# Turning 32 images by 90 degrees: the first group loaded in longer rows and turned like the others

## The chip, the core and the metric

The kernel runs on one core of a Trainium2 chip. The metric is the device time of one execution in microseconds. Three runs of the kernel before took 122.88 to 123.08 us, with a median of 122.94.

## What is computed

```python
def setup_inputs():
    batch, c, h, w = 32, 3, 256, 256
    return {"x": np.random.randn(batch, c, h, w).astype(np.float32)}

def reference(x):
    return np.rot90(x, k=-1, axes=(-2, -1)).astype(np.float32)
```

There are 96 images (32 x 3) of 256 x 256 float32, each turned by a quarter: row i of the result is column i of the image, read from the last row to the first. 25.17 MB come in and 25.17 MB go out, and nothing is calculated.

## The kernel before

**Tiling.** All images together are 24,576 rows of 256 numbers. They are cut into twelve units of 2 MB (128 partitions x 16 rows) and these into five groups, `sizes = (2, 2, 2, 4, 2)` (L38): groups 0, 1, 2 and 4 hold 4 MB each, group 3 holds 8 MB. Each group has a tile `u` of its own in the on-chip memory (L40), which is filled once, turned in place and stored. Nothing is used twice except three small holding areas of 1 MB: `spare[0]` and `spare[1]` in PSUM (L45) and `extra` (L46).

**Loads** are issued on SP's queue, 14 in all. Groups 1 to 4 (L57 to L66) are loaded so that a partition gets whole runs of 16 image rows (32 for group 3), 16 KB (32 KB) in one piece, from each of two halves `a`. A load covers every I-th partition (`to[i::I]`), where I is the group's size: 64 partitions of 128 for I = 2. The last load of the last group is issued as two of 1 MB (L63, L64), and `mark` is the first of them. Group 0 is different (L52 to L56): it is two slabs of 2 MB, in which each partition gets 8 rows, 8 KB, of each of two image sets. Slab 0 comes first, as two loads of 1 MB over all 128 partitions (L55), then slab 1 in one load of 2 MB (L56).

**The turn.** VectorE's transpose swaps blocks of 32 partitions x 32 elements. The loads put an image's rows so that with these blocks and a suitable access pattern the whole quarter turn is done in one pass. Each instruction handles 128 x 2048 elements, and there are 24. In `turn_group` (L80) the tile is split in four quarters (low and high halves of column and row): the first quarter is transposed into a holding area (L88), three more are transposed within the tile, each into the place that the one before it has left (L93), and at the end ScalarE copies the held quarter back (L98). All of them read and write all 128 partitions and both halves `a`. The holding areas are `extra` for group 1, `spare[1]` for group 2, both `spare` for group 3 and `extra` for group 4 (L100). In group 0, `turn_slab` (L68) turns a slab with two transposes: slab 0 into `spare[0]` and `spare[1]` (L75), then slab 1 into the place of slab 0 (L76), and ScalarE copies the two spares into the place of slab 1 (L78).

**Stores** are issued on SP's queue too, two for each group, over the even and the odd partitions (L106 for group 0, L113 for the others): rows of 16 KB, 2 MB each, 4 MB each for group 3.

**The order of the work** is the program's order on each engine; the framework adds the waits that the data need. SP issues all loads and then all stores, in the order of the groups. One dependency is added by hand (L108): the first store waits until the load `mark` has landed, so that stores don't run beside loads, except for the last 1 MB. VectorE takes the groups in order, as do ScalarE's copies.

Of the kernel before, what the change touches and what calls it, by code (L numbers as in the profile page):

```python
# [1 line left out]

# [4 lines left out]


@with_exitstack  # L10
def kernel(
    ctx: ExitStack,
    tc: tile.TileContext,
    x: bass.AP,
    out: bass.AP,
):

    nc = tc.nc
    fp32 = mybir.dt.float32

    B, C, H, W = x.shape
    P = nc.NUM_PARTITIONS
    R = 16  # L30
    E = R * W
    hw = R // 2
    low, high = slice(0, hw), slice(hw, R)

    rows_in = x.rearrange("b c h w -> (b c h) w")
    rows_out = out.rearrange("b c h w -> (b c h) w")

    sizes = (2, 2, 2, 4, 2)  # L38
    first = [sum(sizes[:n]) for n in range(len(sizes))]
    groups = [  # L40
        ctx.enter_context(tc.tile_pool(name=f"group{n}", bufs=1)).tile([P, s, E], fp32, name=f"u{n}")
        for n, s in enumerate(sizes)
    ]
    psum = ctx.enter_context(tc.tile_pool(name="psum", bufs=1, space=bass.MemoryType.PSUM))
    spare = [psum.tile([P, E // 2], fp32, name=f"spare{h}") for h in range(2)]  # L45
    extra = ctx.enter_context(tc.tile_pool(name="extra", bufs=1)).tile([P, E // 2], fp32, name="extra")  # L46

    def rows_of(rows, n):
        return rows[first[n] * P * R : (first[n] + sizes[n]) * P * R]


    ld = rows_of(rows_in, 0).rearrange("(s i p r) w -> s i p (r w)", s=2, i=2, p=P)  # L52
    home = [groups[0][:, s].rearrange("p (i f) -> p i f", i=2) for s in range(2)]
    for i in range(2):
        nc.sync.dma_start(out=home[0][:, i], in_=ld[1, i])  # L55
    nc.sync.dma_start(out=home[1], in_=ld[0].transpose([1, 0, 2]))  # L56
    for n in range(1, len(sizes)):  # L57
        I = sizes[n]
        ld = rows_of(rows_in, n).rearrange("(a i m r) w -> i m a (r w)", a=2, i=I, m=P // I)
        to = groups[n].rearrange("p s f -> p (s f)").rearrange("p (a f) -> p a f", a=2)  # L60
        for i in range(I):
            if (n, i) == (len(sizes) - 1, I - 1):
                mark = nc.sync.dma_start(out=to[i::I, 0], in_=ld[i][:, 0])  # L63
                nc.sync.dma_start(out=to[i::I, 1], in_=ld[i][:, 1])  # L64
            else:
                nc.sync.dma_start(out=to[i::I], in_=ld[i])  # L66

    def turn_slab(src, dsts):  # L68
        s = src.rearrange("p (i r g c) -> p c r g i", i=2, r=R // 2, c=R)
        for h, d in enumerate(dsts):  # L70
            d = d.rearrange("p (c k r) -> p c r k", c=hw, r=R // 2)[:, :, ::-1, ::-1]
            nc.vector.transpose(out=d, in_=s[:, h * hw : (h + 1) * hw])  # L72

    u = groups[0]
    turn_slab(u[:, 0], spare)  # L75
    turn_slab(u[:, 1], [u[:, 0, : E // 2], u[:, 0, E // 2 :]])  # L76
    for h in range(2):
        nc.scalar.copy(out=u[:, 1, h * E // 2 : (h + 1) * E // 2], in_=spare[h])  # L78

    def turn_group(n, held):  # L80
        I = sizes[n]
        T = I // 2
        K = W // (R * T)
        u = groups[n].rearrange("p s f -> p (s f)")
        src = u.rearrange("p (a t r g c) -> p t c r g a", a=2, t=T, r=R, c=R)
        dst = u.rearrange("p (i c k t r) -> p t c r k i", i=I, c=R, k=K, t=T)[:, ::-1, :, ::-1, ::-1, :]
        for t in range(T):
            nc.vector.transpose(  # L88
                out=held[t].rearrange("p (i c k r) -> p c r k i", i=I, c=hw, k=K)[:, :, ::-1, ::-1, :],
                in_=src[:, t, low, low])  # L90
        for c, r in ((low, high), (high, high), (high, low)):
            for t in range(T):
                nc.vector.transpose(out=dst[:, t, c, r], in_=src[:, t, c, r])  # L93
        back = u.rearrange("p (i c k t r) -> p t i c k r", i=I, c=R, k=K, t=T)[:, ::-1]
        for t in range(T):
            kept = held[t].rearrange("p (i c k r) -> p i c k r", i=I, c=hw, k=K)
            for i in range(I):
                nc.scalar.copy(out=back[:, t, i, low, :, high], in_=kept[:, i])  # L98

    for n, held in enumerate(([extra], [spare[1]], spare, [extra]), 1):  # L100
        turn_group(n, held)


    st = rows_of(rows_out, 0).rearrange("(s i m r) w -> i m s (r w)", s=2, i=2, m=P // 2)
    for a in range(2):
        put = nc.sync.dma_start(out=st[a], in_=groups[0][a::2])  # L106
        if a == 0:
            tc.add_manual_dep(put.ins, mark.ins.name, mybir.DependencyInfo(  # L108
                mybir.DependencyClass.Sync, mybir.DependencyReason.SCHED_ONLY), reason="stores after loads")
    for n in range(1, len(sizes)):  # L110
        st = rows_of(rows_out, n).rearrange("(a i m r) w -> a m i (r w)", a=2, i=sizes[n], m=P // 2)
        for a in range(2):
            nc.sync.dma_start(out=st[a], in_=groups[n][a::2])  # L113


# [1 line left out]
_INS = ['x']  # L117
_OUTS = [((32, 3, 256, 256), 'float32')]


# [23 lines left out]
```

## Time and profile before

| | us |
|---|---|
| median of three runs | 122.94 |
| profiled execution, its own time | 122.88 |
| its span, first to last instruction | 121.1 |
| VectorE busy, 24 transposes | 87.4 |
| ScalarE busy, copies and a table load | 14.9 |
| GpSimd busy | 0.2 |
| group 0: two transposes to `spare` (L72) | 7.1 |
| group 0: two transposes within `u` (L72) | 7.8 |
| group 0: two copies from `spare` (L78) | 3.6 |
| issue of one load of 1 MB, 128 rows of 8 KB (L55) | 0.38 to 0.42 |
| issue of one load of 1 MB, 64 rows of 16 KB (L63, L64) | 0.51, 0.50 |
| SP waits for `mark` ahead of the first store (L106) | 31.2 |

TensorE does nothing, and the clock granted is 1.0. The profile's page gives busy time by engine, the span in 40 slices, the DMA queues, the chain that ended last and the costliest groups of instructions. In a line of a group, "L93 DVE ... x15 | 54.4, 3649 | 0.4" means: line 93, VectorE, 15 instructions, 54.4 us in all, 3649 ns for one, 0.4 us of idle time ahead of them. DVE is VectorE, ACT ScalarE, SP the engine whose queue (SPq) issues all transfers here. "mean busy share" of the DMA line is that of 16 DMA engines. An issue on the queue is only the handing over of a transfer; its packets move later, and the trace has a record of each packet (start, duration, size).

### The profile page before, as it was taken

The page shows a single profiled execution, that of the slowest core. Times are in us where ns is not written, and L with a number is a line of the kernel's source. Part 1 is how long each engine was busy: PE and PEld are TensorE (multiplying, and loading weights), DVE is VectorE, ACT ScalarE, POOL GpSimd, SP SyncE. Part 2 cuts the span into 40 slices and gives each one's busy share as a digit, 9 for nine tenths or more (in the row PEclk, how much of TensorE's full clock was granted, in tenths as well). Part 3 has the DMA queues.
Part 4 walks back from the last instruction along what each step waited for, and adds up shares of the span by engine and source line. Part 5 has one row for each costly group of instructions (what it writes and reads, how often), then busy time and mean ns, then how long its engine had stood idle before and what let it go on. Part 6 is the DMA issues. An engine that isn't in the chain of part 4 may idle for free.

```text
span 121.1 us, 131 instructions
## 1 busy us (share of the span) xinstructions
DVE 87.4 (72%) x24; ACT 14.9 (12%) x17; POOL 0.2 (0%) x4
## 2 busy tenths in 40 slices
DVE  0039999999999999999999999999999600000000
ACT  0000400380005100060000000318000330000000
POOL 0000000000000000000000000000000000000000
DMA  2999999999989898999999999999999999999994
GB/s 89 428 428 422 452 433 433 433 433 433 520 346 520 346 520 346 428 422 411 433 433 428 433 433 428 417 417 433 428 433 433 433 433 433 433 433 433 433 422 184
DMA packets 3456, 50.33 MB, mean 416 GB/s; under 512 B 384, under 2 KB 384, under 8 KB 384
## 3 DMA queue, kind: packets, MB, share of 16 engines
q1 hardware_dynamic: 3456, 50.33, 97.6%
HBM read 25.17 MB, written 25.17 MB: 416 GB/s over the span
## 4 chain that ended last, share of the span: by engine, by line
DVE 66%; issue 6%; DMA 6%; ACT 1%; ACTq 1%; SPq 0%; DVEq 0%
DVE u L93 39%; DVE spare L88 9%; DVE extra L88 6%; DVE u L72 6%; DVE spare L72 6%; DMA u<-in_x_dram 6%; ACT u L98 1%; ACTq L139 1%; SPq L55 0%; DVEq L88 0%; DVEq L72 0%
## 5 line engine op out<-in xcount | busy, mean ns | idle before, releaser
L93 DVE STREAM_TRANSPOSE u<-u 128x2048 f32<-128x2048 f32 x15 | 54.4, 3649 | 0.4
L72 DVE STREAM_TRANSPOSE spare<-u 128x2048 f32<-128x2048 f32 x2 | 7.1, 3586 | 8.1 <-DMA u<-in_x_dram 8.1
L98 ACT COPY u<-spare 128x512 f32<-128x512 f32 (+1 forms) x10 | 6.0, 687 | 38.5 <-DVE u L93 38.5
L88 DVE STREAM_TRANSPOSE spare<-u 128x2048 f32<-128x2048 f32 x3 | 10.7, 3588 | 0.0
L72 DVE STREAM_TRANSPOSE u<-u 128x2048 f32<-128x2048 f32 x2 | 7.8, 3988 | 0.0
L88 DVE STREAM_TRANSPOSE extra<-u 128x2048 f32<-128x2048 f32 x2 | 7.8, 3896 | 0.0
L98 ACT COPY u<-extra 128x1024 f32<-128x1024 f32 x4 | 4.0, 1043 | 22.8 <-DVE u L93 22.8
L78 ACT COPY u<-spare 128x2048 f32<-128x2048 f32 x2 | 3.6, 1870 | 8.7 <-DVE u L72 8.7
L78 ACT ACT_TABLE_LOAD x1 | 1.3, 1283 | 13.0 <-DMA u<-in_x_dram 13.0
L128 POOL MEMSET const-uint8-127<- 128x1 uint8 x1 | 0.1, 103 | 0.0
L128 POOL MEMSET const-bfloat16-1.0<- 128x1 bf16 x1 | 0.1, 102 | 0.0
L128 POOL MEMSET const-float32-0.0<- 128x1 f32 x1 | 0.1, 99 | 0.2 <-issue 0.2
L128 POOL MEMSET const-float32-1.0<- 128x1 f32 x1 | 0.1, 99 | 0.0
## 6 DMA issues: line engine op xcount, KB each, us to landing
u<-in_x_dram SPq DMA_DIRECT2D x10, 2048.0 KB, 30.4
out_dram<-u SPq DMA_DIRECT2D x8, 2048.0 KB, 18.2
out_dram<-u SPq DMA_DIRECT2D x2, 4096.0 KB, 21.1
u<-in_x_dram SPq DMA_DIRECT2D x4, 1024.0 KB, 20.5
```

Source lines behind the costliest of these rows:

```text
L72: nc.vector.transpose(out=d, in_=s[:, h * hw : (h + 1) * hw])
L78: nc.scalar.copy(out=u[:, 1, h * E // 2 : (h + 1) * E // 2], in_=spare[h])
L88: nc.vector.transpose(out=held[t].rearrange("p (i c k r) -> p c r k i", i=I, c=hw, k=K)[:, :, ::-1, ::-1, :], in_=src[:, t, low, low])
L93: nc.vector.transpose(out=dst[:, t, c, r], in_=src[:, t, c, r])
L98: nc.scalar.copy(out=back[:, t, i, low, :, high], in_=kept[:, i])
L128: nc = _bacc.Bacc("TRN2", target_bir_lowering=False, num_devices=1)
L139: with _tile.TileContext(nc) as tc:
```

## The change

Group 0 loses its own layout, its own turn and its own stores, and goes through the code of the other groups. Its loads are rows of 16 KB on every second partition: the first half `a` of the even partitions (1 MB, 64 partitions), the second half of them (1 MB), and the odd partitions (2 MB). It is turned by `turn_group` with `spare[0]` as the holding area: one transpose to `spare[0]`, three within the tile, two copies of 128 x 1024 by ScalarE. The dependency on `mark` moves into the common loop of stores.

```diff
-    ld = rows_of(rows_in, 0).rearrange("(s i p r) w -> s i p (r w)", s=2, i=2, p=P)
-    home = [groups[0][:, s].rearrange("p (i f) -> p i f", i=2) for s in range(2)]
-    for i in range(2):
-        nc.sync.dma_start(out=home[0][:, i], in_=ld[1, i])
-    nc.sync.dma_start(out=home[1], in_=ld[0].transpose([1, 0, 2]))
-    for n in range(1, len(sizes)):
+    for n in range(len(sizes)):
         I = sizes[n]
         ld = rows_of(rows_in, n).rearrange("(a i m r) w -> i m a (r w)", a=2, i=I, m=P // I)
         to = groups[n].rearrange("p s f -> p (s f)").rearrange("p (a f) -> p a f", a=2)
         for i in range(I):
-            if (n, i) == (len(sizes) - 1, I - 1):
+            if (n, i) in ((0, 0), (len(sizes) - 1, I - 1)):
                 mark = nc.sync.dma_start(out=to[i::I, 0], in_=ld[i][:, 0])
                 nc.sync.dma_start(out=to[i::I, 1], in_=ld[i][:, 1])
             else:
                 nc.sync.dma_start(out=to[i::I], in_=ld[i])
-
-    def turn_slab(src, dsts):
-        s = src.rearrange("p (i r g c) -> p c r g i", i=2, r=R // 2, c=R)
-        for h, d in enumerate(dsts):
-            d = d.rearrange("p (c k r) -> p c r k", c=hw, r=R // 2)[:, :, ::-1, ::-1]
-            nc.vector.transpose(out=d, in_=s[:, h * hw : (h + 1) * hw])
-
-    u = groups[0]
-    turn_slab(u[:, 0], spare)
-    turn_slab(u[:, 1], [u[:, 0, : E // 2], u[:, 0, E // 2 :]])
-    for h in range(2):
-        nc.scalar.copy(out=u[:, 1, h * E // 2 : (h + 1) * E // 2], in_=spare[h])
...
-    for n, held in enumerate(([extra], [spare[1]], spare, [extra]), 1):
+    for n, held in enumerate(([spare[0]], [extra], [spare[1]], spare, [extra])):
         turn_group(n, held)
...
-    st = rows_of(rows_out, 0).rearrange("(s i m r) w -> i m s (r w)", s=2, i=2, m=P // 2)
-    for a in range(2):
-        put = nc.sync.dma_start(out=st[a], in_=groups[0][a::2])
-        if a == 0:
-            tc.add_manual_dep(put.ins, mark.ins.name, ...)
-    for n in range(1, len(sizes)):
+    for n in range(len(sizes)):
         st = rows_of(rows_out, n).rearrange("(a i m r) w -> a m i (r w)", a=2, i=sizes[n], m=P // 2)
         for a in range(2):
-            nc.sync.dma_start(out=st[a], in_=groups[n][a::2])
+            put = nc.sync.dma_start(out=st[a], in_=groups[n][a::2])
+            if (n, a) == (0, 0):
+                tc.add_manual_dep(put.ins, mark.ins.name, ...)
```

## The prediction

> **What bounds the kernel now.** I read the page first: busy time, the line of the DMA engines in 40 slices, the queue, and the groups of instructions.
>
> ```profile
> span 121.1 us, 131 instructions
> ## 1 busy us (share of the span) xinstructions
> DVE 87.4 (72%) x24; ACT 14.9 (12%) x17; POOL 0.2 (0%) x4
> ...
> DMA  2999999999989898999999999999999999999994
> ...
> q1 hardware_dynamic: 3456, 50.33, 97.6%
> ...
> L93 DVE STREAM_TRANSPOSE u<-u 128x2048 f32<-128x2048 f32 x15 | 54.4, 3649 | 0.4
> ```
>
> The DMA engines are full from the second slice to the last: 97.6% of 121.1 us is 118.2 us of packets. VectorE has 87 us of work, starts late and is done 25 us before the end. So the time is start-up, plus 118 us of transfer, plus an end, plus any moment in which the queue runs dry. There is none now. The chain that ended last gives VectorE 66%; that is how stores are linked back to transposes and not what sets the end, since after the last copy at 97.9 us the DMA engines still move for 22 us.
>
> The windows view (length, then busy time of VectorE, ScalarE and GpSimd, clock, DMA share, GB/s) shows start and steady state:
>
> ```profile
> 0.73:1.73 1.00, 0.00 (x0) 0.00 (x0) 0.00 (x0) 1.00 0.00 0
> 1.73:2.38 0.65, 0.00 (x0) 0.00 (x0) 0.00 (x0) 1.00 0.37 50
> 2.38:2.90 0.52, 0.00 (x0) 0.00 (x0) 0.00 (x0) 1.00 0.88 347
> 2.90:12.20 9.30, 4.13 (x2) 0.00 (x0) 0.00 (x0) 1.00 1.01 428
> 14.00:31.00 17.00, 16.90 (x6) 3.92 (x3) 0.00 (x0) 1.00 1.01 432
> ```
>
> The first issue is at 0.73 us, the first packets at 1.73, all sixteen engines run from about 2.8. The 8 KB rows (2.9 to 12.2 us) go at 428 GB/s, the 16 KB rows after them at 432 (431 in the same view from 62 to 90 us, for stores). Last come the timelines of VectorE and of the queue on SP (start, length), which show how early each step is done:
>
> ```profile
> 8.06 7.08 DVE L72 STREAM_TRANSPOSE spare<-u 128x2048 f32<-128x2048 f32 x2 [8.06 <-DMA u<-in_x_dram]
> 15.18 7.82 DVE L72 STREAM_TRANSPOSE u<-u 128x2048 f32<-128x2048 f32 x2
> 22.84 3.91 DVE L88 STREAM_TRANSPOSE extra<-u 128x2048 f32<-128x2048 f32 x1
> 26.78 10.93 DVE L93 STREAM_TRANSPOSE u<-u 128x2048 f32<-128x2048 f32 x3
> 37.60 3.59 DVE L88 STREAM_TRANSPOSE spare<-u 128x2048 f32<-128x2048 f32 x1
> 41.23 10.93 DVE L93 STREAM_TRANSPOSE u<-u 128x2048 f32<-128x2048 f32 x3
> 52.12 7.08 DVE L88 STREAM_TRANSPOSE spare<-u 128x2048 f32<-128x2048 f32 x2
> ```
>
> ```profile
> 59.43 1.37 SPq L106 DMA_DIRECT2D out_dram<-u  x2
> ...
> 84.25 2.06 SPq L113 DMA_DIRECT2D out_dram<-u  x2
> ```
>
> VectorE never rests from 8.06 to 95.9 us (its transposes sat idle 0.4 us in all ahead of L93, the last column above), so whatever delays its start delays every later group. The 8 MB of group 3 are ready at 84.2 us, and its store is issued at 84.25.
>
> **The change, part by part.**
>
> *Bytes and rows.* The loads of group 0 stay three, of 1, 1 and 2 MB, so the queue, its 14 loads, its 10 stores and the order of their waits stay. Only the packets differ: 512 of 8 KB become 256 of 16 KB. The trace's packet records have 309 ns for the one and 613 for the other; 512 x 309 / 16 = 9.89 us against 256 x 613 / 16 = 9.81. That is on the path: **-0.08 us**.
>
> *Start-up.* SP issues the first load in 377 ns (L55, 128 rows of 8 KB); the same form as the new one, 64 rows of 16 KB on every second partition, is L63 and L64, with 505 and 495. If the first packet waits for the issue to end, everything is 0.12 us later. On the other side, the sixteen engines get their first packets from 1.73 to 2.80 us, four at once and twelve from 2.39; if that spread is the time in which 128 rows are described, 64 rows would need half of it, and the last engine would start 0.5 us earlier. The bounds are -0.5 and +0.2 us (two such issues). I take **+0.12**, since it is a duration of the very form, and what the spread is made of isn't shown.
>
> The Trainium skill speaks against the shape: "DMA: Bandwidth & Descriptors", Rules for kernel authors, wants 128 partitions for full bandwidth and says that transfers to disjoint halves of the partitions aren't worth splitting. Here the loads after 14 us are all of 64 or 32 partitions and move 432 GB/s, more than the 428 of the 128-partition loads; by the rule the first 4 MB would be slower, by these rows they aren't, and the rows decide.
>
> *ScalarE.* Two copies of 128x2048 out of PSUM (1.87 us each) go, two of 128x1024 (1.01 us on the same kind of tile) come. ScalarE is 12% busy and group 0's stores wait until 59.4 us for the loads in any case: nothing. Without that cover a copy would count a microsecond.
>
> *VectorE: the start.* Now the first transpose needs slab 0 alone, the first two loads; it starts at 8.06 us, 0.1 after they have landed. The in-place turn reads all 128 partitions and both halves of the row in its first transpose, so it needs all three loads, which have landed at 12.94 (ScalarE's first wait and SP's next issue end there). VectorE starts at 13.04. Behind that wait stand all 24 transposes. Their number stays. Group 0 then has the form of group 2 (one transpose into PSUM, three in place), which takes 52.12 - 37.60 = 14.52 us, so group 1 begins at 27.56 instead of 22.84: **4.7 us later**, with data there since 22.5. Nothing later makes it up, as VectorE has no idle time. The buffers don't add a wait: spare[0] is free again by 31 us and next wanted at 57, spare[1] keeps its two users and their distance.
>
> *Who waits for that.* Groups 0, 1 and 2 are ready at about 30, 45 and 59 us; their stores go out from 59.43, held by the loads. Group 2 is fourth to sixth in line (63.8 and later): covered. Group 4 is ready at 102.6 instead of 97.9 and its packets begin at 109.9: covered by 7 us. **Group 3** is the one to look at. Its store is issued at 84.25 + 4.71 = 88.96 us. The packets before it end at 90.33 on the first engine and 90.49 on the last (loads end at 61.1 to 61.3; 12.58 MB of stores at 431 GB/s are 29.2 us). Now the store is there 6.1 us ahead; after the change 1.37 to 1.53 us. (What shifts all transfers alike shifts landing and need alike, and drops out.)
>
> Is that enough to feed sixteen engines? No store in this trace meets an idle queue, so the price is bounded. From below: zero, if issue to packet is like the first packet of the whole kernel, 1.73 - 0.73 = 1.0 us. From above: the last engine at the start got its packet 2.80 - 0.73 = 2.07 us after the issue, which would leave 2.07 - 1.37 = 0.7 us dry; with an issue of 0.64 us rather than 0.38, about 0.95. A closer row is the turn from loads to stores: the first store was issued at 59.43, and every engine went from its last load straight on to it at 61.0 to 61.3, with 10 ns between. So a store reaches each engine within 1.57 to 1.83 us, and the most that can be missing by that row is 1.83 - 1.37 = 0.46. I take the late side of this row, as twelve of sixteen engines took 1.66 us and more at the start: 1.66 to 1.83 against 1.37 to 1.53, **+0.3 us**. It is not caught up, since each engine is full from there to the end.
>
> The Trainium skill gives some 0.6 us to the first byte for a transfer issued by SP ("DMA: Bandwidth & Descriptors", Latency and other measured facts). Added to an issue of 0.64 us that would be an estimate of 1.24 us, so no gap at all and about 122.9; this trace's 1.0 us for the first four engines agrees with it, and its 1.66 to 2.07 for the others doesn't.
>
> *Sum.* -0.08 + 0.12 + 0.3 = +0.34 on the profiled execution's 122.88 us (span 121.1 and 1.8 around it) gives 123.2; the median of the runs shown is 0.06 higher. I say **123.25 us**, 0.25% slower.
>
> **The rivals.**
> - *The gap doesn't open.* The store needs under 1.37 us. For it: the first four engines' 1.0. Then 122.94 + 0.04 = **123.0**, no measurable change. 0.2% (0.25 us) is about what a measurement of this kernel can tell.
> - *The gap is wide.* From idle, a 4 MB store of 256 rows costs what the first load did, and more for its longer issue: 0.7 to 0.95 us, so **123.7 to 123.9**. Against it: the turn at 61 us.
> - *Faster.* Half the rows to describe bring the last engines to work 0.5 us sooner at the start, and the gap stays shut: 122.94 - 0.08 - 0.5 = **122.4**. It decides from the point at which the start gains more than 0.2 us over what is lost at 90 us. For it: the spread of 1.07 us at the start is real. Against it: the first packets take 764 to 1176 ns instead of 309, so the first data come no sooner whatever is described, and any gap eats the gain (then no change).
> - *It doesn't do what it says.* If the first transpose waited for half the group only, VectorE would start at 8.06 as now, and only -0.08 + 0.12 would be left: 123.0. The access pattern speaks against it.
>
> **How the numbers follow.** My forecast (a gap of 0.2 to 0.46 us) 0.47, of which a fifth falls short of 0.2%; no gap (with the last rival) 0.25; the wide gap 0.15; the start faster 0.13, of which most is eaten or under 0.25 us. Slower by over 0.2%: 0.8 x 0.47 + 0.15 = 0.52. Faster by over 0.2%: 0.09. Within: 0.39. The range is 122.75 (start gains, no gap) to 123.9 (a gap of 0.9): what lies outside is about 0.1 on the low side and 0.05 above.
>
> **What would show it.** VectorE's first transpose at 13.0 us, group 3's store issued near 89.0, ScalarE's last copy near 102.6; a dip in the DMA line around 90 us, of 0.3 us on the slowest engines, and none elsewhere; first packets near 1.85 us. I am wrong if the DMA line has no dip there, or if the first 4 MB take longer or shorter by more than 0.2 us, or if the store is issued before 88.5 us.

## The result, and the profile after

The changed kernel takes 123.47 us (median of 5 runs, 123.36 to 123.59) against 122.97 us before. The ratio is 1.0037, with a 95% interval of 1.0023 to 1.0051: half a microsecond slower. The profiled execution took 123.59 us, 0.71 more than the profiled one of before (122.88). Of the five runs of each kernel these are the slowest of the changed one and the fastest of the kernel before, so 0.2 us of the 0.71 belong to the choice of executions and not to the change.

From its page: packets are fewer, their busy share is nearly the same (97.5% for 97.6%), and VectorE's first transpose waits 13.5 us instead of 8.1.

```profile
span 121.8 us, 131 instructions
## 1 busy us (share of the span) xinstructions
DVE 86.9 (71%) x24; ACT 13.2 (11%) x17; POOL 0.2 (0%) x4
...
DMA  4999999999999999999999999999999999999994
...
q1 hardware_dynamic: 3200, 50.33, 97.5%
...
L74 DVE STREAM_TRANSPOSE u<-u 128x2048 f32<-128x2048 f32 x18 | 65.4, 3650 | 0.5
L69 DVE STREAM_TRANSPOSE spare<-u 128x2048 f32<-128x2048 f32 x4 | 14.2, 3581 | 13.5 <-DMA u<-in_x_dram 13.5
```

The windows that the prediction shows of the kernel before, now of the changed one (length; busy VectorE, ScalarE, GpSimd; clock; DMA share; GB/s). A packet is booked whole at its start, so in short windows the share can pass 1:

```profile
0.73:1.73 1.00, 0.00 (x0) 0.00 (x0) 0.00 (x0) 1.00 0.00 0
1.73:2.38 0.65, 0.00 (x0) 0.00 (x0) 0.00 (x0) 1.00 1.80 353
2.38:2.90 0.52, 0.00 (x0) 0.00 (x0) 0.00 (x0) 1.00 0.15 63
2.90:12.20 9.30, 0.00 (x0) 0.00 (x0) 0.00 (x0) 1.00 0.97 410
14.00:31.00 17.00, 16.90 (x5) 2.67 (x3) 0.00 (x0) 1.00 1.00 429
```

Here the reader is to see that almost no packet starts between 2.38 and 2.90 us: fourteen engines began a 16 KB packet at 2.14 to 2.37 us and needed 1.08 to 1.57 us for it. Before, the first 8 KB packets came at 1.73.

VectorE's timeline, with the queue's at the start and at group 3's store:

```profile
13.51 3.60 DVE L69 STREAM_TRANSPOSE spare<-u 128x2048 f32<-128x2048 f32 x1 [13.51 <-DMA u<-in_x_dram]
17.14 10.93 DVE L74 STREAM_TRANSPOSE u<-u 128x2048 f32<-128x2048 f32 x3
27.97 3.87 DVE L69 STREAM_TRANSPOSE extra<-u 128x2048 f32<-128x2048 f32 x1
31.88 10.93 DVE L74 STREAM_TRANSPOSE u<-u 128x2048 f32<-128x2048 f32 x3
```

```profile
0.73 0.60 SPq L56 DMA_DIRECT2D u<-in_x_dram  x1
1.39 0.57 SPq L57 DMA_DIRECT2D u<-in_x_dram  x1
...
89.22 1.28 SPq L87 DMA_DIRECT2D out_dram<-u  x2
```

VectorE is late as forecast, and group 3's store is issued at 89.22 us. But no pause follows: the packets ahead of it end at 90.71 to 91.20, and on each engine the next follows within 10 ns. The first issue takes 0.60 us (0.38 before).

Where the 0.71 us of the profiled executions lie can be read from the small packet that closes each transfer on each engine. These are means over the sixteen engines, after minus before:

| | us |
|---|---|
| end of the first load | +0.42 |
| from there to the end of all loads | -0.10 |
| from there to the end of all stores | +0.23 |
| the last engine behind the mean, at the end | +0.16 |

### The profile page after: what moved, and what is told of

It reads as the page before. It is cut to its first block, busy times and chain, and to the rows that moved or that the text cites. A ratio compares the mean times of both kernels' runs of the same rounds, so it can differ in the third digit from the quotient of the medians.

```text
span 121.8 us, 131 instructions
## 1 busy us (share of the span) xinstructions
DVE 86.9 (71%) x24; ACT 13.2 (11%) x17; POOL 0.2 (0%) x4
## 3 DMA queue, kind: packets, MB, share of 16 engines
q1 hardware_dynamic: 3200, 50.33, 97.5%
## 4 chain that ended last, share of the span: by engine, by line
DVE 60%; issue 12%; DMA 9%; SPq 1%; ACT 1%; ACTq 1%; DVEq 0%
DVE u L74 42%; DVE spare L69 12%; DMA u<-in_x_dram 9%; DVE extra L69 6%; ACT u L79 1%; ACTq L116 1%; SPq L56 0%; SPq L57 0%; DVEq L69 0%
## 5 line engine op out<-in xcount | busy, mean ns | idle before, releaser
L74 DVE STREAM_TRANSPOSE u<-u 128x2048 f32<-128x2048 f32 x18 | 65.4, 3650 | 0.5
L69 DVE STREAM_TRANSPOSE spare<-u 128x2048 f32<-128x2048 f32 x4 | 14.2, 3581 | 13.5 <-DMA u<-in_x_dram 13.5
L79 ACT COPY u<-spare 128x512 f32<-128x512 f32 (+1 forms) x12 | 8.0, 743 | 51.7 <-DVE u L74 51.7
L79 ACT ACT_TABLE_LOAD x1 | 1.3, 1283 | 13.5 <-DMA u<-in_x_dram 13.5
```

The lines of the kernel that those rows point to most:

```text
L69: nc.vector.transpose(out=held[t].rearrange("p (i c k r) -> p c r k i", i=I, c=hw, k=K)[:, :, ::-1, ::-1, :], in_=src[:, t, low, low])
```

## The experiments

Three theories stood at the start. **The start**: the form of the first loads costs. **The late turn**: VectorE's delay lets the queue run dry at group 3. **The rest**: something in the store phase.

**1. VectorE late, loads as before** (late_vector). From the kernel before:

```diff
-        nc.sync.dma_start(out=home[0][:, i], in_=ld[1, i])
-    nc.sync.dma_start(out=home[1], in_=ld[0].transpose([1, 0, 2]))
+        nc.sync.dma_start(out=home[1][:, i], in_=ld[0, i])
+    nc.sync.dma_start(out=home[0], in_=ld[1].transpose([1, 0, 2]))
```

> The kernel before, with the two 1 MB loads filling slab 1 and the 2 MB load filling slab 0, which is turned first. The three loads keep their form, size and order on the queue, and only VectorE starts later, at about 13.0 us instead of 8.06. If the loss lies in the first microseconds of the transfers (theory of the start), the first packets come at 1.73 us as before and the time is 122.97 us within 0.15. If it lies in VectorE's late start (theory of the late turn: group 3's store meets a queue that is nearly dry), the time is 123.3 to 123.5 us and the packets pause near 90 us.

123.05 us against 123.03, ratio 1.0001 (0.9992 to 1.0010). VectorE starts at 13.01 us, 4.95 later than before, and group 3's store goes out at 89.03 us:

```profile
13.01 7.08 DVE L72 STREAM_TRANSPOSE spare<-u 128x2048 f32<-128x2048 f32 x2 [13.01 <-DMA u<-in_x_dram]
...
85.97 3.03 ACT L98 COPY u<-spare 128x512 f32<-128x512 f32 x6 [2.67 <-DVE u L93]
89.03 1.28 SPq L113 DMA_DIRECT2D out_dram<-u  x2
```

The packets ahead end at 90.33 to 90.51, and the new ones follow without a pause. The theory of the late turn falls: this delay alone costs nothing that can be measured.

**2. VectorE later still** (later_vector): the same, and one more transpose ahead.

```diff
+    for _ in range(1):
+        nc.vector.transpose(out=extra, in_=u[:, 0, : E // 2])
     turn_slab(u[:, 0], spare)
```

> The kernel before with the late start of late_vector and one more transpose of 128x2048 into the holding area extra ahead of all others, whose result is not used: VectorE is 8.8 us later than in the kernel before, and group 3's store is issued near 93.0 us, 2.6 us after the packets ahead of it have run out near 90.4. Both theories: a gap then opens, of 2.6 us and the time from an issue to its packets on an idle queue, which no trace has shown for a store. If that is 1.0 us as for the first packets of the kernel, 126.6 us; if it is 1.5 us, 127.1 us; if it is 2.07 us as for the last engines of the first load, 127.6 us.

125.13 us, ratio 1.0167 (1.0153 to 1.0181). The extra transpose took 2.31 us and not 3.9, so the store was issued at 91.33, not 93.0:

```profile
13.13 2.31 DVE L76 STREAM_TRANSPOSE extra<-u 128x2048 f32<-128x2048 f32 x1 [13.13 <-DMA u<-in_x_dram]
...
91.33 1.26 SPq L115 DMA_DIRECT2D out_dram<-u  x2
```

Now the queue does run dry. The windows of this kernel and then of the changed one:

```profile
88.00:90.45 2.45, 2.45 (x2) 2.17 (x5) 0.00 (x0) 1.00 1.00 428
90.45:92.59 2.14, 2.10 (x2) 0.86 (x2) 0.00 (x0) 1.00 0.00 0
92.59:96.00 3.41, 3.38 (x2) 0.00 (x0) 0.00 (x0) 1.00 1.10 461
```

```profile
88.00:90.45 2.45, 2.42 (x2) 1.19 (x3) 0.00 (x0) 1.00 1.02 428
90.45:92.59 2.14, 2.14 (x1) 0.00 (x0) 0.00 (x0) 1.00 0.95 398
92.59:96.00 3.41, 3.38 (x2) 0.00 (x0) 0.00 (x0) 1.00 1.04 442
```

Nothing starts for 2.1 us, and 2.1 us is what the kernel loses. The packets of the store start on all sixteen engines between 92.59 and 92.74 us, **1.26 to 1.41 us after its issue**. That is the price on an idle queue that no earlier trace had shown. In late_vector the store is issued at 89.03 us and the engines want it at 90.33 to 90.51, a margin of 1.30 to 1.48 us; in the changed kernel the margin is 1.49 us on the first engine. Both just made it. By these numbers, an estimate, a tenth or two more of delay would have begun to show.

**3. Which part of the first loads costs?** Four edits of group 0's loads in the changed kernel, and four of the first loads in the kernel before. First 8 KB rows on the 64 even partitions (after_8k):

```diff
-            if (n, i) in ((0, 0), (len(sizes) - 1, I - 1)):
+            if (n, i) == (0, 0):
+                nc.sync.dma_start(out=to[i::I, :, : E // 2], in_=ld[i][:, :, : E // 2])
+                nc.sync.dma_start(out=to[i::I, :, E // 2 :], in_=ld[i][:, :, E // 2 :])
+            elif (n, i) == (len(sizes) - 1, I - 1):
```

> The changed kernel, with the first two loads cut between the halves of a row instead of between a = 0 and 1: again 64 even partitions and 1 MB each, but 128 rows of 8 KB instead of 64 rows of 16 KB. Theory of the start, if the long first packets are its cost: first packets take well under 1 us, the third load lands at 13.1 to 13.2 us instead of 13.46, and the time is 123.0 to 123.2 us. Theory of the start, if the 64 partitions and the longer issue (0.60 us) are its cost: 123.4 us or more, since twice the rows are described. Theory of the late turn: 123.4 to 123.5 us, as VectorE still starts at 13 us.

Then 128 partitions, 8 KB rows (after_128x8k):

```diff
+        if n == 0:
+            ld = rows_of(rows_in, 0).rearrange("(a p r) w -> a p (r w)", a=2, p=P)
+            for h in range(2):
+                nc.sync.dma_start(out=to[:, 0, h * E // 2 : (h + 1) * E // 2], in_=ld[0][:, h * E // 2 : (h + 1) * E // 2])
+            nc.sync.dma_start(out=to[:, 1], in_=ld[1])
+            continue
```

> The changed kernel, with group 0 loaded over all 128 partitions: two loads of 1 MB in rows of 8 KB, then 2 MB in rows of 16 KB. Rows of group 0 land on other partitions than the turn supposes, so group 0's part of the output is not the reference's; instructions and sizes of the turn and the stores are those of the changed kernel. Theory of the start: issue 0.4 us, first packets at 1.73 us, 122.9 to 123.1 us, whatever in the first load's form it is. Theory of the late turn: 123.4 to 123.5 us.

64 neighbouring partitions, 16 KB rows (after_64near), and 128 partitions, 16 KB rows (after_128x16k), are the same edit with these loads in the place of its own:

```diff
+            for h in range(2):
+                nc.sync.dma_start(out=to[h * P // 2 : (h + 1) * P // 2, 0], in_=ld[0][h * P // 2 : (h + 1) * P // 2])
+            nc.sync.dma_start(out=to[:, 1], in_=ld[1])
```

> The changed kernel, whose first two loads fill the 64 neighbouring partitions 0 to 63 and then 64 to 127 (1 MB each, 64 rows of 16 KB, a megabyte in one piece in memory as in the changed kernel), then 2 MB over 128 partitions. Group 0's rows land on other partitions than the turn supposes, so its part of the output is not the reference's. Two theories of what costs 0.4 us at the start. The step of two partitions: with neighbours the issue falls from 0.60 us to 0.4, first packets come at 1.75 us, and the time is 123.0 to 123.1 us. The 64 partitions: issue and first packets stay as in the changed kernel (0.60 us, 2.1 us) and the time is 123.4 to 123.6 us. A Trainium skill page (SBUF - State Buffer, Door 1: the DMA port swizzle) has partitions 0 to 63 on half the ports; by it the packets of these two loads would last about twice as long (1.2 us for 613 ns) and 4.8 us would be lost, an estimate; no run so far shows such a load.

```diff
+            for h in range(2):
+                nc.sync.dma_start(out=to[:, h], in_=ld[h])
```

> The changed kernel, whose group 0 is loaded in two loads of 2 MB over all 128 partitions in rows of 16 KB. Group 0's rows land on other partitions than the turn supposes, so its part of the output is not the reference's. The length of the row is then alone with the size of the load. If neither costs, as the run with 8 KB rows on 64 partitions suggests, the issue takes 0.4 us, first packets come at 1.75 us, and the time is 123.0 to 123.1 us. If the long first packets cost on their own, the third packet wave is 0.2 us later and the time is 123.2 to 123.3 us.

In the kernel before: one first load of 2 MB (before_one), the second load on ScalarE's queue (before_act), rows of 4 KB (before_4k), and a first load of 32 partitions (before_32):

```diff
-    for i in range(2):
-        nc.sync.dma_start(out=home[0][:, i], in_=ld[1, i])
+    nc.sync.dma_start(out=home[0], in_=ld[1].transpose([1, 0, 2]))
```

> The kernel before, with the first two loads of 1 MB in one of 2 MB, 256 rows of 8 KB. It parts the two things that the run with 16 KB rows on 128 partitions changed at once. If the size of the first load costs, 123.3 to 123.4 us as there; if the length of the row does, 123.0 us, first packets at 1.75 us and short.

```diff
-        nc.sync.dma_start(out=home[0][:, i], in_=ld[1, i])
+        (nc.sync, nc.scalar)[i].dma_start(out=home[0][:, i], in_=ld[1, i])
```

> The kernel before, with the second 1 MB load issued by ScalarE's queue instead of SP's, so that both first loads are handed over at the same time. If the start is limited by how fast loads are handed over and described, the sixteen engines have packets earlier than 2.8 us and 0.1 to 0.4 us are won: 122.6 to 122.9 us. If it is limited by the way to the first data, or both queues share what describes, 123.0 us. If the two queues' packets alternate, slab 0 lands at 7.9 us as now and nothing later changes.

```diff
-    for i in range(2):
-        nc.sync.dma_start(out=home[0][:, i], in_=ld[1, i])
+    for h in range(2):
+        cut = slice(h * E // 4, (h + 1) * E // 4)
+        nc.sync.dma_start(out=home[0][:, 0, cut], in_=ld[1, 0][:, cut])
+    nc.sync.dma_start(out=home[0][:, 1], in_=ld[1, 1])
```

> The kernel before, with the first 1 MB load cut in two of 0.5 MB, 128 rows of 4 KB each. If the first wave costs by the length of its packets (8 KB: 0.2 us of excess over all engines in the first 4 us, 16 KB on the same 128 partitions: 0.8), 4 KB win 0.1 to 0.2 us: 122.8 to 122.9 us, which would beat both kernels. If each load has a cost of its own at the start, or 4 KB packets are slower in themselves, 123.1 us or more.

```diff
-    for i in range(2):
-        nc.sync.dma_start(out=home[0][:, i], in_=ld[1, i])
+    for q in (slice(0, 32), slice(32, P)):
+        nc.sync.dma_start(out=home[0][q, 0], in_=ld[1, 0, q])
+    nc.sync.dma_start(out=home[0][:, 1], in_=ld[1, 1])
```

> The kernel before, with the first load cut in 32 and 96 partitions (0.25 and 0.75 MB in rows of 8 KB), two packets for each engine in the first. If the spread of the first packets (1.73 to 2.80 us) is the time in which 128 rows are described, 32 rows are described in a quarter of it, all engines start by 2.1 us and 0.3 us are won: 122.7 us. If the issue of the second load, 0.4 us behind, is then late for the engines, they pause at 2.4 us and the time stays at 123.0 us. If each load has a fixed start of its own, 123.1 us or more.

All together, with the length of the first issue, the start of the first packet, and the time at which the first 2 MB are in (mean of the engines, from one trace each):

| kernel | first load | issue us | first packet at | 2 MB in at | ratio to before (95%) |
|---|---|---|---|---|---|
| before | 128 partitions x 8 KB | 0.38 | 1.74 | 7.46 | 1 |
| late_vector | the same | 0.38 | 1.75 | 7.42 | 1.0001 (0.9992 to 1.0010) |
| after_128x8k | the same | 0.38 | 1.75 | 7.58 | 1.0002 (0.9993 to 1.0011) |
| before_act | the same, on two queues | 0.39 | 1.76 | 7.66 | 1.0016 (1.0007 to 1.0024) |
| before_one | 2 MB, 256 rows of 8 KB | 0.43 | 1.84 | 7.73 | 1.0020 (1.0010 to 1.0029) |
| after_128x16k | 2 MB, 128 rows of 16 KB | 0.37 | 1.74 | 7.67 | 1.0035 (1.0023 to 1.0048) |
| after | 64 even partitions x 16 KB | 0.60 | 2.14 | 7.90 | 1.0037 (1.0023 to 1.0051) |
| after_8k | 64 even partitions, 2 x 8 KB | 0.73 | 2.27 | 7.95 | 1.0039 (1.0027 to 1.0052) |
| before_4k | 0.5 MB, 128 x 4 KB | 0.38 | 1.74 | 8.01 | 1.0075 (1.0063 to 1.0088) |
| before_32 | 0.25 MB, 32 partitions x 8 KB | 0.40 | 1.77 | 8.77 | 1.0137 (1.0121 to 1.0152) |
| after_64near | 64 neighbours x 16 KB | 0.59 | 2.11 | 11.96 | 1.0406 (1.0391 to 1.0420) |

The last column compares medians of 4 to 11 runs. The column before it has single traces: later_vector, with the loads of late_vector, has its first 2 MB in at 7.58 us, so traces of one form lie between 7.42 and 7.58.

The first issue and VectorE's start in after_128x8k, and then the first issues of after_8k and after_64near:

```profile
0.73 0.38 SPq L57 DMA_DIRECT2D u<-in_x_dram  x1
13.30 3.61 DVE L75 STREAM_TRANSPOSE spare<-u 128x2048 f32<-128x2048 f32 x1 [13.30 <-DMA u<-in_x_dram]
...
0.73 0.73 SPq L56 DMA_DIRECT2D u<-in_x_dram  x1
...
0.73 0.59 SPq L57 DMA_DIRECT2D u<-in_x_dram  x1
```

What follows:

- after_128x8k has the changed turn, the changed stores and VectorE's late start, and nothing of the loss (1.0002). **The loss comes with the changed loads of group 0.** The theory of the start stands.
- No run shows the length of the row as the cause: 8 KB rows on 64 partitions are as slow as 16 KB rows (1.0039, where 1.000 to 1.002 was expected if long rows were the cause). That pair isn't clean, as after_8k's first issue is also longer (0.73 us for 0.60); before_one and after_128x16k, both with 2 MB first, differ in the row alone at the start, have 7.73 and 7.67 us there, and their ratios' intervals overlap.
- The issue is long (0.59 to 0.73 us) and the first packet late (2.1 to 2.3 us) in each kernel whose first load has 64 partitions, evens or neighbours, and in none with 128 or 32. So it isn't the step of two. In the changed kernel the first packet is 0.40 us later and the first 2 MB are in 0.44 us later. That the one makes the other is likely but not shown by itself, since the next point has a loss without late packets. Why handing over a first load on 64 partitions takes longer than one on 128 is open.
- A first load of 2 MB, or two of 1 MB at once, also costs: 0.2 to 0.4 us in the medians (1.0016 to 1.0035), with rows of 8 KB as with 16 KB, although it is handed over about as early as before. At the first 2 MB these three are 0.1 to 0.3 us behind the traces of the old form. In before_act sixteen engines that all start at once don't get data sooner: they start at 1.76 to 1.95 us, and their first packets last 0.75 to 1.23 us.
- Small first packets don't help, against what I expected of before_4k: early packets of 4 KB often last 0.3 to 0.5 us instead of 0.16, so from 2.38 to 3.50 us the engines are as busy but move 230 GB/s where 8 KB rows move 395. The kernel also has one load more, and the run doesn't part the two.
- Which partitions a load covers matters more than anything else here. after_64near at its first two loads, and with the other loads later, in two windows:

```profile
2.00:11.60 9.60, 0.00 (x0) 0.00 (x0) 0.00 (x0) 1.00 1.03 222
14.00:31.00 17.00, 12.83 (x4) 0.55 (x1) 0.00 (x0) 1.00 1.01 432
```

The same share of busy time moves half the data: packets of 16 KB last 1.25 us instead of 0.61. The Trainium skill ("SBUF — State Buffer", Door 1: The DMA port swizzle) has partitions 0 to 63 on 8 of 16 ports and 64 to 127 on the other 8, which would be some 218 GB/s for each of the two loads; the run agrees with 222 in this window. Every second partition of 128 doesn't have this cost, as the 432 GB/s of the later groups show. The 32 and 96 partitions of before_32 may be a case of the same kind, which no run tests: its 8 KB packets last about 0.51 us instead of 0.31 from 3 to 5 us.

No version of the start beat the kernel before.

**4. The store phase.** Most kernels with the changed group 0 lost another 0.2 us in the profile after the loads. The one edit left was where group 0's stores go in memory. In the changed kernel and in the kernel before, in turn:

```diff
+        order = "(a i m r) w -> a m i (r w)" if n else "(i a m r) w -> a m i (r w)"
-        st = rows_of(rows_out, n).rearrange("(a i m r) w -> a m i (r w)", a=2, i=sizes[n], m=P // 2)
+        st = rows_of(rows_out, n).rearrange(order, a=2, i=sizes[n], m=P // 2)
```

> The changed kernel, in which group 0's two stores go to memory in the pattern of the kernel before: the two 16 KB rows of a partition 2 MB apart instead of 1 MB, so group 0's images come out at other places than the reference has them. In the profiles, kernels with the changed group 0 lose a further 0.2 us between the turn to stores at 61 us and the end, most of it while group 0's and 1's stores run; kernels with the old group 0 don't. Theory of the store pattern: that part goes, and 123.2 to 123.3 us are left, by the start alone (0.3 us). Theory that it is an effect of the start or of chance: 123.4 to 123.5 us as the changed kernel.

```diff
-    st = rows_of(rows_out, 0).rearrange("(s i m r) w -> i m s (r w)", s=2, i=2, m=P // 2)
+    st = rows_of(rows_out, 0).rearrange("(i s m r) w -> i m s (r w)", s=2, i=2, m=P // 2)
```

> The kernel before, in which group 0's two stores go to memory in the pattern of the changed kernel: the two 16 KB rows of a partition 1 MB apart instead of 2 MB, so group 0's images come out at other places than the reference has them. Theory of the store pattern: 0.2 us are lost between 61 and 90 us, 123.2 us. Theory of the start or of chance: 123.0 us, packets between 61 and 90 us as in the kernel before.

after_oldstore: 123.42 us, ratio 1.0035 (1.0023 to 1.0048). before_newstore: 122.97 us, ratio 0.9996 (0.9987 to 1.0005). The theory of the store pattern falls on both sides.

What the traces do show: from the mean end of the loads to the mean end of the stores it takes 58.68 to 58.76 us in before, before_newstore, late_vector, before_act, before_32 and after_64near, 58.85 to 58.96 in after, after_oldstore, after_8k, after_128x8k, after_128x16k and before_one, and 59.10 in before_4k. So it isn't the changed turn and stores of group 0: after_64near has them without this loss (58.68), and before_one has the loss without them. Nor is it simply how far apart the engines are at the end of the loads: 0.53 us in before_act and 0.67 in later_vector, which loses nothing up to group 3, but 0.32 in after_oldstore, which loses. Where the time goes can be seen, though not why: from 1 to 10 us after the loads the packets of 16 KB last 618 ns on average in the changed kernel, and 611 to 612 in before, late_vector and after_64near.

One small part is an engine with nothing to do. The first store waits for `mark`, it reaches the engines 1.33 us after its issue (59.85 to 61.18 us in the changed kernel), and by then the earliest engine has been dry for 0.07 us, which is 0.01 on the mean of the engines. In before_4k eight of sixteen engines have run dry by then, the earliest for 0.53 us, 0.1 on the mean.

All these are single executions, which differ by 0.2 us between runs of one kernel. after_128x8k has 58.90 us here and no loss in its median, and the profiled executions of before, late_vector and before_newstore were the fastest of theirs. So how much of the 0.2 us is real is open, and so is its cause.

## Why the prediction was right in the time and wrong in the place

- **Bound.** Right: the transfers set the end, and each loss that could be placed lies there: an engine for transfers waited for its first data or had nothing to move, or its packets took longer.
- **Rows of 16 KB**, -0.08 us: the loads after the first win 0.10 us on the mean of the engines, which fits.
- **Start-up**, +0.12: this is the term that was mis-sized, and it carries the result. The end of the first load is 0.42 us later. I took the new form's issue from L63 and L64, late in the kernel, 0.50 us; as the first transfer it takes 0.60. And I let the first packet move by the issue's growth alone (0.22 by these numbers), while it came 0.40 us later: 0.81 us after the issue's end instead of 0.62. The upper bound of +0.2 was too low too. The rows that I let decide about 64 partitions were of loads after 14 us: they hold for the rate (429 GB/s there in the changed kernel) and say nothing of a first load. The four engines at once and twelve from 2.39 us, on which the lower bound and the late side of the price at group 3 stood, are of one execution: with the same first load late_vector has eight engines at work by 1.82 us, before_newstore twelve by 2.01, and neither is faster for it.
- **VectorE's shift**, 4.71 us: group 1 begins 5.13 us later (27.97 for 22.84), which is the forecast and the late start of the loads. That nothing makes it up was right; group 4's cover of 7 us held.
- **The gap at group 3**, +0.3 us: it didn't open. The margin was right (1.37 to 1.53 us in the forecast, 1.49 for the first engine as it came), and the price was wrong: 1.26 to 1.41 us measured, 1.66 to 1.83 assumed. The step that failed was to take an upper bound as the value. That every engine had its store within 1.57 to 1.83 us at the turn at 61 us only showed that it came no later, since the engines were still busy; the row that measured, though of the start, was the 1.0 us of the first four engines. The Trainium skill's 0.6 us to the first byte ("DMA: Bandwidth & Descriptors", Latency and other measured facts), added to the 0.60 us that the issue took in later_vector, gives an estimate of 1.20 us, and the run agrees to within a tenth on the first engine (1.26). Of the rivals, "the gap doesn't open" had the right mechanism here, with 123.0 us, and failed by the start.
- **The rest**, +0.2 us in the store phase of the profiled execution, no step of mine had foreseen; its cause is open, and so is how much of it is the choice of executions.
- The sum, 123.25, lies half-way from the kernel before to the measured 123.47 because a start too cheap by 0.3 us and a gap too dear by 0.3 us cancelled. That the time fell near it was luck. The signs I had named tell them apart at once, and two of those for being wrong came: no dip at 90 us, and the first 4 MB in 0.5 us later (13.46 for 12.94), with first packets at 2.1 us and not 1.85.

## What to carry to other kernels

Where transfers are the bound from the first microsecond to the last, look first at what the very first transfer looks like: here other forms of it cost 0.2 to 4.9 us of 123 (0.5 in the changed kernel), and nothing later made that up. It isn't priced by the same form in the middle of the kernel. A delay of another engine costs nothing until a transfer is issued later than the queue's end less the time from issue to first packet (here 1.26 to 1.41 us for a store), and from there every microsecond counts. An interval within which something must have happened, because nobody was seen to wait, is a bound and not a duration.

## What the runs showed of the hardware

- The first packets of a kernel are slow on many engines. In the kernel before, the 8 KB packets of the four engines that start first last 0.76 to 1.18 us, those of the other twelve 0.31 to 0.44, and 0.31 later. In the changed kernel fourteen of the first sixteen 16 KB packets last 1.08 to 1.57 us, 0.61 later. It is over within about 2 us.
- A load of 64 partitions as the first of the kernel: issue 0.59 to 0.73 us, first packet at 2.10 to 2.27; of 128 or 32: 0.37 to 0.43 and 1.74 to 1.84.
- A store of 4 MB on an idle queue: first packets 1.26 to 1.41 us after its issue.
- 64 neighbouring partitions: 222 GB/s; 64 partitions with a step of two: 429 to 432.
- A transpose of 128x2048 whose source and target are both read and written in order takes 2.31 us, against 3.6 to 4.0 us for the same size with the access patterns of the turn.
